# Tensor work of GpSimd before the first feed-forward moved to VectorE, in a two-block transformer kernel

## The chip, the cores and the metric

The kernel runs on one core of a Trainium2 chip. The metric is the device time of one execution in microseconds (us). Engines are named as in the profile: PE (matrix engine), PEld (its weight loads), DVE (VectorE), ACT (ScalarE), POOL (GpSimd), SP (issues most of the DMAs).

## The reference, cut

Two blocks work on 256 tokens of width 2048 in float32. What follows is the part around the change: the state-space mixer and the gated sum of the first block.

```python
def _s5_mixer(u, a_re, a_im, log_dt, b_re, b_im, c_re, c_im, d, w_glu):
    dt = jnp.exp(log_dt.astype(f32))[:, None]
    mag = jnp.exp(a_re * dt)
    abar_re = mag * jnp.cos(a_im * dt)
    abar_im = mag * jnp.sin(a_im * dt)
...
    bbar_re = z_re[..., None] * b_re - z_im[..., None] * b_im
    bbar_im = z_re[..., None] * b_im + z_im[..., None] * b_re
...
    y = (jnp.einsum('sbgn,gcn->bsgc', h_re, c_re.astype(f32))
         - jnp.einsum('sbgn,gcn->bsgc', h_im, c_im.astype(f32))
         + d.astype(f32) * uf)
    y = jax.nn.gelu(y.reshape(B, S, SSM_WIDTH))
    return y * jax.nn.sigmoid(y @ w_glu.astype(f32))

def first_block(...):
    cond = jax.nn.silu(c)
    mod = cond @ w_ada[i] + b_ada[i]
    shift1, scale1, gate1, shift2, scale2, gate2 = jnp.split(mod, N_MOD, axis=-1)
    h = _modulate(_rms(x, norm1_w[i]), shift1, scale1).astype(x.dtype)
    u, q, k, v = jnp.split(h @ w_in[i], splits, axis=-1)
    y_ssm = _s5_mixer(u, ...)
    y_att = _dilated_attention(q, k, v, q_norm_w[i], k_norm_w[i])
    mixed = jnp.concatenate([y_ssm, y_att], axis=-1).astype(x.dtype) @ w_out[i]
    x = x + gate1[:, None, :] * mixed
    h2 = _modulate(_rms(x, norm2_w[i]), shift2, scale2).astype(x.dtype)
    ffn = (jax.nn.silu(h2 @ w_ffn_gate[i]) * (h2 @ w_ffn_up[i])) @ w_ffn_down[i]
    return x + gate2[:, None, :] * ffn
```

The second block (neighbourhood attention, latent attention, attention to a memory of 256 tokens, a second feed-forward) follows; the keys and values of the memory are computed at the very start.

## The kernel before

All weights are streamed once, as tiles of 1 MB in one fixed order (`fl.order`), by SP into six buffers `r`. There are two kinds. A tile of kind "w" holds four chunks of 128 rows by 512 columns; it is split into a high and a low float32r part, in two halves: ACT writes `h` (L207), then `l = r - h` is made (L208). Four buffers each of `h` and `l`, of half a tile, stand between the splitters and PE. Each tile then costs PE 24 matmuls of 512 columns (`mm3`: L221, L222 with `h`, L226 with `l`). A tile of kind "a" is one of 96 tiles of `w_ada`; DVE alone takes it, with two multiply-adds into `acc` (L950), and PE needs it only when a half vector is done.

`Flow.run` sets the program order. For each "w" tile it emits the split of both halves, then the matmuls of an earlier tile, then one step of every open task (`fl.step`): the state-space tables (`s_prep`, at a rate of 1, later 2, then 3 steps per tile), the runs of the state-space sections (`s_run`), attention heads, norms and the ends of column groups. The schedule is manual, so every engine works through its own list in the order in which this code emits it, and waits at the head of its list.

Before the first feed-forward (some 84 "w" tiles and 84 "a" tiles) `Flow.share` says how many halves of a "w" tile get their low part on POOL: none for the memory's keys and values, then `(1,0)`, one half of every second tile, then `(1,)`, one half of every tile, up to the feed-forward, which has `(0,)`.

In the same stretch POOL makes the state-space tables in `Ssm.prep`, for each of eight sections: products of B and C with powers (L627, which read tables that ACT fetches), their sums into `X` and `C` (L635), three doublings of the rotation table `E` (`double`, L609 to L612; its first eight columns, `E8`, are made the same way once for all sections), the diagonal `dI` (L682), a zeroed `T` (L685). PE transposes `X` (L672), ACT copies the result (L673) and the first eight columns of `E` (L676), which the doublings then read. In `out1`, POOL multiplies the attention half of the output projection by the gate (L1194) and adds it to x (L1197). Further POOL work: zeroing `acc` (L945), ahead of a small DMA that ACT issues (L946), and the powers that make each reciprocal root (L299).

Of the kernel before, what the change touches and what calls it, by code (L numbers as in the profile page):

```python
# [13 lines left out]
OP = mybir.AluOpType  # L14
AX = mybir.AxisListType
PSUM = bass.MemoryType.PSUM
# [7 lines left out]
SP = 4  # L24
# [4 lines left out]
# ---------------------------------------------------------------- layout on the host  # L29
# [119 lines left out]
# ---------------------------------------------------------------- the program  # L149

class Core:
# [26 lines left out]
    # -- tiles  # L178
# [23 lines left out]
    def split_half(self, r, i, shared):  # L202
        """two float32r parts of two chunks of 128 rows of a weight tile of four"""
        nc = self.nc
        h, l = [self.wp.tile([128, 2, r.shape[-1]], F32R, name=self.nm(n), tag=n, bufs=self.NW) for n in "hl"]
        r = r[:, 2 * i:2 * i + 2]
        nc.scalar.activation(h, r, AF.Copy)  # L207
        (nc.gpsimd if shared else nc.vector).tensor_tensor(l, r, h.bitcast(F32), op=OP.subtract)  # L208
        return h, l

    def mm3(self, ps, acts, parts, first, last, ts=(0, 1)):
        """ps[t] += acts.T @ weights over two chunks; acts: [(h, l)], parts: (h, l) of the weights"""
        nc = self.nc
        if not isinstance(ps, list):
            ps = [ps[:, t] for t in range(2)]
        h, l = parts
        n = h.shape[-1]
        for k, (ah, al) in enumerate(acts):
            for t in ts:
                s = slice(t * 128, (t + 1) * 128)  # L220
                nc.tensor.matmul(ps[t][:, :n], al[:, s], h[:, k], start=first and k == 0, stop=False)  # L221
                nc.tensor.matmul(ps[t][:, :n], ah[:, s], h[:, k], start=False, stop=False)  # L222
        for k, (ah, al) in enumerate(acts):
            for t in ts:
                s = slice(t * 128, (t + 1) * 128)
                nc.tensor.matmul(ps[t][:, :n], ah[:, s], l[:, k], start=False,  # L226
                                 stop=last and k == len(acts) - 1)

    # -- to channel-major
    def tr4(self, src, k, dg=None):  # L230
        """chunks k, k+1 of token-major src (two tiles of [128, 512]) -> PSUM [128, 2, 256];
        dg: a diagonal matrix of factors for each token half"""
        ps = self.pm((128, 2, 256))
        for j in range(2):
            for t in range(2):
                o, i = ps[:, j, t * 128:(t + 1) * 128], src[t][:, (k + j) * 128:(k + j + 1) * 128]
                if dg is None:
                    self.nc.tensor.transpose(o, i, self.ident)  # L238
                else:
                    self.nc.tensor.matmul(o, i, dg[t], start=True, stop=True)  # L240
        return ps
# [4 lines left out]
    def chunks(self, src, n=4, w=None, ab=None, dg=None):  # L246
        """token-major src -> n chunks (h, l) of [128 channels, 256 tokens]; w(k): a factor per
        channel, ab(k): a factor and an offset per channel"""
        nc = self.nc
        out = []  # L250
        for k in range(0, n, 2):
            ps = self.tr4(src, k, dg)
            h, l = self.acts2()
            if w is None and ab is None:
                self.split(ps, h, l)
            for j in range(2):
                if w is not None:
                    self.split(ps[:, j], h[:, j], l[:, j], w(k + j))
                elif ab is not None:
                    a, b = ab(k + j)  # L260
                    f = self.up.tile([128, 256], F32, name=self.nm("f"), tag="f", bufs=3)
                    nc.scalar.activation(h[:, j], ps[:, j], AF.Identity, scale=a, bias=b)
                    nc.scalar.activation(f, ps[:, j], AF.Identity, scale=a, bias=b)
                    nc.vector.tensor_tensor(l[:, j], f, h[:, j].bitcast(F32), op=OP.subtract)
                out.append((h[:, j], l[:, j]))
        return out
# [10 lines left out]
    def plain(self, src, w=1.0, new=None):  # L277
        """token-major src -> two float32 tiles [128, 2, 256] of two chunks each"""
        out = []
        for k in (0, 2):  # L280
            ps = self.tr4(src, k)
            o = (new or self.unit)((128, 2, 256))
            self.nc.scalar.activation(o, ps, AF.Copy, scale=w)
            out.append(o)
        return out

    # -- norms
# [5 lines left out]
    def rstd(self, ss, n, width, out=None):  # L293
        """(ss / width + eps) ** -0.5 of n columns"""
        nc = self.nc
        r = self.small(n) if out is None else out
        m = self.small(n)
        nc.vector.tensor_scalar(m, ss, 1.0 / width, EPS, op0=OP.mult, op1=OP.add)  # L298
        nc.gpsimd.tensor_tensor(r, m, self.mhalf[:, :n], op=OP.pow)  # L299
        return r  # L300
# [6 lines left out]
    # -- attention pieces  # L307
    def softmax(self, src, scale):
        """src [128 queries, 2, 256 keys] -> normalised probabilities of softmax(scale * src)"""
        nc = self.nc  # L310
# [12 lines left out]
    def flip(self, p, parts=False):  # L323
        """probabilities -> [128 keys, 2, 256 queries], or two float32r parts of that"""
        nc = self.nc
# [13 lines left out]
    def values(self, ps, v, c, pt):  # L339
        """ps [128 channels, 256 queries] = v[:, c-th 128 columns].T @ probabilities"""  # L340
        for s in range(2):
            self.nc.tensor.matmul(ps, v[s][:, c * 128:(c + 1) * 128], pt[:, s], start=s == 0, stop=s == 1)  # L342


class Flow:
    """Streams the weight tiles in a fixed order, loads ahead, and steps the other tasks in between."""
# [36 lines left out]
    def run(self, main, other):  # L383
        """main: a generator that takes a split weight tile at each step; other[kind]: one that takes a raw tile"""
# [36 lines left out]
def pipeline(gens):  # L421
    """starts a generator at each step, with the earlier ones a step further"""
# [14 lines left out]
# ---------------------------------------------------------------- state space mixer  # L437

class Ssm:
# [17 lines left out]
    def params(self):  # L457
        """[128, 32] tables of one value per state; on VectorE and GpSimd"""
# [143 lines left out]
    def double(self, E, pr, steps):  # L602
        """powers of the rotation, from n = 2 ** i of them to twice as many: E[n:2n] = E[0:n] * ph[i]"""
        G, m = self.k.nc.gpsimd, E.shape[2]
# [12 lines left out]
    def prep(self, s):  # L617
        """the section's matmul operands and rotation tables"""
        k, nc, pool = self.k, self.k.nc, self.pool
        G, A = nc.gpsimd, nc.scalar  # L620
# [4 lines left out]
        def products(o, a, b):  # L625
            """a * b for four values b per state, a [128, SP, 16] -> a compact [128, SP, 4, 16]"""
# [4 lines left out]
        def combine(o, u, v, op):  # L631
            """each group of a pair to its own channels"""
# [52 lines left out]
        G.memset(T, 0.0)  # L685
# [6 lines left out]
    def finish(self):  # L692
        """the matmuls of the section whose tables were made last"""
# [18 lines left out]
    def run(self, s, u4, ytok):  # L712
        """u4 [128 (q, channel), SP, 64]; ytok: two views [128, 32 * SP], gelu(y) token-major"""
# [40 lines left out]
# ---------------------------------------------------------------- the two blocks  # L754

def build(ctx, tc, A, out):
# [23 lines left out]
    # ---- the order of the weight tiles  # L780
# [8 lines left out]
    def mixed(ws, as_, lag=0, lead=0):  # L789
        """weight tiles with the others spread evenly among all but the first and last of them"""  # L790
# [52 lines left out]
    # ---- groups of 512 columns  # L843
    open_ps = {}

    def group(acts, done, kbs, key=None, first=True, last=True, half=None):
        """takes a weight tile for each of kbs; acts[kb]: its four chunks, once there; then done(ps) is a task,
        or half(ps, t) ends each token half"""
# [18 lines left out]
    def tok(ps, r=None, n=512, base=None, new=unit):  # L867
        """a group's PSUM to two token-major tiles, times r per token, or added to those of base"""
# [15 lines left out]
    # ---- start: the memory, the input's norm  # L884
# [19 lines left out]
    def s_mem():  # L904
        """steps with the first weight tiles"""
# [31 lines left out]
    # ---- modulation  # L937
# [3 lines left out]
    def s_ada():  # L941
        """takes the tiles of w_ada in the order of W: 8 of two chunks to a half of a vector"""
# [42 lines left out]
    def modulate(xs, g, i, dg=None):  # L985
        """chunks of (x * r) * md[i + 1] + md[i] of the column group"""
# [27 lines left out]
    # ---- block 1: projections  # L1014
# [114 lines left out]
    # ---- block 1: state space mixer  # L1129
# [45 lines left out]
    # ---- block 1: output and feed-forward  # L1175
# [6 lines left out]
    def out1(g, i):  # L1182
        def done(ps):
            if i == 0:
                part[g] = tok(ps)
            elif i == 1:
# [6 lines left out]
                for t in range(2):  # L1193
                    G.tensor_tensor(part[g][t], part[g][t], gate[2][g], op=OP.mult)  # L1194
                yield
                for t in range(2):
                    G.tensor_tensor(x[g][t], x[g][t], part[g][t], op=OP.add)  # L1197
# [69 lines left out]
    # ---- block 2: mixers  # L1267
# [14 lines left out]
    def apply_rope(src, dst, nh, t):  # L1282
        """src, dst [128, nh, 64]"""
# [165 lines left out]
    # ---- block 2: memory attention  # L1449
    def parts(src, shape=(128, 2, 256)):  # L1450
        """a tile in two float32r parts"""
# [67 lines left out]
    def half2(ps, t):  # L1519
        """the last sum of a token half, and its norm"""  # L1520
# [16 lines left out]
    # ---- the program  # L1537
    fn = []

    def main():  # L1540
# [10 lines left out]
        fl.share = (1,0)  # L1551
# [13 lines left out]
        fl.share = (1,)  # L1565
# [73 lines left out]
```

## Time and profile before

| | us |
|---|---|
| median of 3 runs | 2764.36 (2763.05 to 2769.06) |
| span of the profiled execution | 2763.5 |
| PE busy | 2641.9 (96%) |
| DVE busy | 1665.0 (60%) |
| ACT busy | 1259.9 (46%) |
| POOL busy | 452.3 (16%) |
| chain that ended last: PE, POOL, DVE | 80%, 7%, 5% |

Busy times are averages over stages that differ: POOL's work lies nearly all in the first 750 us. The mean of a group of instructions includes any time in which an instruction had begun and was held up. Rows of waits name who ended the wait, not who caused it to be late. The profiled execution's span and the median differ by 0.9 us.

### The profile page before, as it was taken

Reading aid. Unit: us, or ns where it says so; the run is one execution under the profiler, and the core shown is the slowest. Engines: PE = TensorE matmul, PEld = TensorE weight load, DVE = VectorE, ACT = ScalarE, POOL = GpSimd, SP = SyncE. Lnnn points to the kernel's source line nnn. Section 1 sums busy time; section 2 is a strip of 40 time slices with the busy share of each in tenths; the row PEclk is TensorE's granted clock in tenths of the full one; section 3 lists DMA queues with packets and bytes.
Section 4 is the critical chain, followed back from the end, with each engine's and each line's share of the span. In section 5 each row is a group of like instructions: output and inputs, shape, how many; then the busy total and the mean of one; then the engine's idle time right before and its main releaser. Section 6 shows DMA issues by size and latency. Waiting matters only on the chain.

```text
span 2763.5 us, 31609 instructions
## 1 busy us (share of the span) xinstructions
PE 2641.9 (96%) x12272; PEld 2195.8 (79%) x12272; DVE 1665.0 (60%) x1834; ACT 1259.9 (46%) x1786; POOL 452.3 (16%) x409
## 2 busy tenths in 40 slices
PE   7879888888899999999999999999999999999998
PEld 6768777776788888888888878888888888888887
DVE  7967878769767554455456454665554454454445
ACT  5354445553544443433445455454454344443434
POOL 2470198827400000000000011100000000000001
PEclk9989999989999999999999999999999999999999
DMA  8978666557577555555545543455455555555552
GB/s 333 358 260 327 230 234 218 198 211 275 207 312 277 211 184 197 195 186 197 184 178 181 192 141 134 171 188 193 182 199 183 196 196 185 198 184 198 183 187 103
DMA packets 90030, 577.97 MB, mean 209 GB/s; under 512 B 9996, under 2 KB 12428, under 8 KB 22680
## 3 DMA queue, kind: packets, MB, share of 16 engines
q1 hardware_dynamic: 80928, 561.61, 55.2%
q10 hardware_dynamic: 8952, 14.34, 1.6%
q8 instruction: 96, 1.57, 0.2%
q14 instruction: 54, 0.44, 0.1%
HBM read 569.63 MB, written 6.29 MB: 208 GB/s over the span
## 4 chain that ended last, share of the span: by engine, by line
PE 80%; POOL 7%; DVE 5%; issue 3%; ACT 3%; DMA 1%; SPq 0%; ACTq 0%; POOLq 0%; DVEq 0%
PE g L226 25%; PE g L221 24%; PE g L222 24%; PE m L238 2%; DVE l L208 1%; POOL v L627 1%; DVE acc L950 1%; POOL l L208 1%; ACT h L207 1%; POOL C L635 1%; POOL X L635 1%; POOL v L609 1%; POOL v L610 1%; POOL u L1197 0%; POOL u L611 0%
## 5 line engine op out<-in xcount | busy, mean ns | idle before, releaser
L208 DVE TENSOR_TENSOR l<-r,h 128x1024 fp32r<-128x1024 f32 (+1 forms) x832 | 1025.9, 1266 | 587.9 <-ACT h L207 581.9
L221 PE MATMUL g<-h,u 128*128 128x512 f32 x3424 | 1357.1, 396 | 10.3 <-ACT h L207 8.2
L222 PE MATMUL g<-h,u 128*128 128x512 f32 x3424 | 1340.8, 392 | 0.0
L207 ACT ACTIVATE h<-r 128x1024 fp32r<-128x1024 f32 x866 | 884.6, 1056 | 668.7 <-PE g L222 601.0
L226 PE MATMUL g<-l,u 128*128 128x512 f32 x3424 | 924.4, 392 | 58.5 <-DVE l L208 39.6
L226 PEld LDWEIGHTS g<-l,u 128*128 128x128 f32 x3424 | 643.3, 189 | 204.4 <-DVE l L208 49.9
L221 PEld LDWEIGHTS g<-h,u 128*128 128x128 f32 x3424 | 650.4, 190 | 146.3 <-ACT h L207 10.9
L222 PEld LDWEIGHTS g<-h,u 128*128 128x128 f32 x3424 | 650.0, 190 | 132.9 <-issue 1.0
L950 DVE SCALAR_TENSOR_TENSOR acc<-r,cond,acc 128x1024 f32<-128x1024 f32 x192 | 280.6, 1461 | 3.6
L299 POOL TENSOR_TENSOR r<-s,mhalf 128x2 f32<-128x2 f32 x5 | 3.5, 702 | 894.8 <-DVE s L298 894.8
L208 POOL TENSOR_TENSOR l<-r,h 128x1024 fp32r<-128x1024 f32 x34 | 95.3, 2805 | 169.1 <-ACT h L207 164.9
L1515 POOL TENSOR_TENSOR u<-u,w 128x512 f32<-128x512 f32 x6 | 7.7, 1297 | 698.7 <-ACT j L291 698.7
L271 ACT ACTIVATE u<-m 128x512 fp32r<-128x512 f32 (+1 forms) x80 | 42.7, 574 | 162.8 <-PE m L238 128.3
L291 ACT ACTIVATE j<-u 128x512 bf16<-128x512 f32 (+2 forms) x92 | 47.3, 514 | 123.8 <-DVE u L1208 36.7
L272 DVE TENSOR_TENSOR u<-m,u 128x512 fp32r<-128x512 f32 (+1 forms) x80 | 50.0, 658 | 86.2 <-ACT u L271 86.2
L238 PE MATMUL m<-ident,u 128*128 128x128 f32 x372 | 53.3, 287 | 25.3 <-ACT u L982 11.9
L274 ACT ACTIVATE u<-m,vec 128x256 fp32r<-128x256 f32 x86 | 38.9, 472 | 72.7 <-PE m L342 30.5
L238 PEld LDWEIGHTS m<-ident,u 128*128 128x128 f32 x372 | 45.7, 148 | 32.7 <-ACT u L982 13.6
L275 DVE SCALAR_TENSOR_TENSOR u<-m,vec,u 128x256 fp32r<-128x256 f32 x86 | 40.0, 481 | 44.4 <-ACT u L274 44.3
L320 POOL TENSOR_TENSOR u<-u,s 128x512 f32<-128x512 f32 x20 | 20.8, 1042 | 265.4 <-DVE s L319 265.4
L1255 DVE TENSOR_TENSOR w<-g,w 128x512 f32<-128x512 f32 x24 | 16.5, 687 | 43.4 <-PE g L226 43.4
L1239 DVE SCALAR_TENSOR_TENSOR w<-g,r,w 128x512 f32<-128x512 f32 x22 | 15.5, 747 | 44.4 <-PE g L226 44.4
(238 smaller groups left out, 1438.5 us busy)
## 6 DMA issues: line engine op xcount, KB each, us to landing
r<-in_w_ada_dram SPq DMA_DIRECT2D x96, 1024.0 KB, 5.3
r<-in_wg_dram SPq DMA_DIRECT2D x88, 1024.0 KB, 4.8
r<-in_wu_dram SPq DMA_DIRECT2D x88, 1024.0 KB, 4.8
r<-in_wd_dram SPq DMA_DIRECT2D x88, 1024.0 KB, 4.8
r<-in_w_in_dram SPq DMA_DIRECT2D x32, 1024.0 KB, 4.9
r<-in_w_out_dram SPq DMA_DIRECT2D x32, 1024.0 KB, 6.1
r<-in_w_qkv_dram SPq DMA_DIRECT2D x24, 1024.0 KB, 4.8
r<-in_w_xk_dram SPq DMA_DIRECT2D x16, 1024.0 KB, 9.4
```

The costliest lines, as they stand in the source:

```text
L207: nc.scalar.activation(h, r, AF.Copy)
L208: (nc.gpsimd if shared else nc.vector).tensor_tensor(l, r, h.bitcast(F32), op=OP.subtract)
L221: nc.tensor.matmul(ps[t][:, :n], al[:, s], h[:, k], start=first and k == 0, stop=False)
L222: nc.tensor.matmul(ps[t][:, :n], ah[:, s], h[:, k], start=False, stop=False)
L226: nc.tensor.matmul(ps[t][:, :n], ah[:, s], l[:, k], start=False, stop=last and k == len(acts) - 1)
L238: self.nc.tensor.transpose(o, i, self.ident)
L271: nc.scalar.activation(h, ps, AF.Copy)
L272: nc.vector.tensor_tensor(l, ps, h.bitcast(F32), op=OP.subtract)
L275: nc.vector.scalar_tensor_tensor(l, ps, w, h.bitcast(F32), op0=OP.mult, op1=OP.subtract)
L291: self.nc.scalar.activation(j[:, :n], src, AF.Square, accum_out=acc)
L635: G.tensor_tensor(o[r, :, :, 16 * q:16 * q + 16], u[r], v[r], op=op)
L950: V.scalar_tensor_tensor(acc, r[:, j], cond[:, 2 * kb + j:2 * kb + j + 1], acc, op0=OP.mult, op1=OP.add)
```

## The change

Four edits. `split_half` keeps its branch, but `fl.share` is now `(0,)` in both places, so that DVE makes every low part. `double` and `prep` bind `G` to VectorE in place of GpSimd; zeroing `T` stays on GpSimd. In `out1` the gate's product and the sum go from `G` to `V`. Comments and docstrings are dropped as well.

```diff
     def double(self, E, pr, steps):
-        G, m = self.k.nc.gpsimd, E.shape[2]
+        G, m = self.k.nc.vector, E.shape[2]
...
     def prep(self, s):
         k, nc, pool = self.k, self.k.nc, self.pool
-        G, A = nc.gpsimd, nc.scalar
+        G, A = nc.vector, nc.scalar
...
         T = k.unit((128, SP, 128))
-        G.memset(T, 0.0)
+        nc.gpsimd.memset(T, 0.0)
...
                 for t in range(2):
-                    G.tensor_tensor(part[g][t], part[g][t], gate[2][g], op=OP.mult)
+                    V.tensor_tensor(part[g][t], part[g][t], gate[2][g], op=OP.mult)
                 yield
                 for t in range(2):
-                    G.tensor_tensor(x[g][t], x[g][t], part[g][t], op=OP.add)
+                    V.tensor_tensor(x[g][t], x[g][t], part[g][t], op=OP.add)
...
         m_acts.clear()
-        fl.share = (1,0)
+        fl.share = (0,)
         prep[1] = 3
...
             yield from group(mixed_acts, out1(g, 0), (2,))
-        fl.share = (1,)
+        fl.share = (0,)
         for g in range(2):
```

PE's and ACT's lists stay the same, word for word. On DVE, in the middle of the projections, this is where one section's rotation table is doubled (`u_4568` is that section's `E`, `csl` and `snl` are cosines and sines, `l` a low part):

```order
 L950 SCALAR_TENSOR_TENSOR acc_4052<-r_4355,cond,acc_4052 128x1024 x2
 L208 TENSOR_TENSOR l_4536<-r_4359,h_4535 128x1024
+L208 TENSOR_TENSOR l_4540<-r_4359,h_4539 128x1024
+L609 TENSOR_TENSOR v_4570<-u_4568,csl 128x64
+L610 TENSOR_TENSOR v_4571<-u_4568,snl 128x64
+L611 TENSOR_TENSOR u_4568<-v_4570,v_4571 128x4x8
+L612 TENSOR_TENSOR u_4568<-v_4570,v_4571 128x4x8
+L609 TENSOR_TENSOR v_4576<-u_4568,csl 128x128
+L610 TENSOR_TENSOR v_4577<-u_4568,snl 128x128
```

The second half's low part and the doublings now stand in DVE's list, between one tile's low parts and the next; L609 there waits for ACT's copy L676, as it did on POOL.

On POOL, this is the place of the first norm's reciprocal root (`r_107`, L299), between two sections' tables:

```order
-L612 TENSOR_TENSOR u_1615<-v_1671,v_1672 128x4x32
-L682 TENSOR_TENSOR v_1677<-i_119,ssm_p 128x128
 L685 MEMSET u_1679 128x512
 L299 TENSOR_TENSOR r_107<-s_1687,mhalf 128x2
-L627 TENSOR_TENSOR v_1731<-u_1729,wr 128x256
-L627 TENSOR_TENSOR v_1732<-u_1729,wi 128x256
-L635 TENSOR_TENSOR X<-v_1731,v_1732 64x16x16 x2
-L627 TENSOR_TENSOR v_1813<-u_1729,wi 128x256
-L627 TENSOR_TENSOR v_1814<-u_1729,wr 128x256
-L635 TENSOR_TENSOR X<-v_1813,v_1814 64x16x16 x2
 L945 MEMSET acc_1876 128x1024
```

Only the zeroing of `T` and `acc` and the root remain there.

On DVE, at the end of the output projection (`u_5325`, `u_5327` are x, the other `u` parts and gates, `g_5369` a group's PSUM):

```order
 L208 TENSOR_TENSOR l_5393<-r_5265,h_5392 128x1024
+L208 TENSOR_TENSOR l_5397<-r_5265,h_5396 128x1024
+L1197 TENSOR_TENSOR u_5325<-u_5325,u_4680 128x512
+L1197 TENSOR_TENSOR u_5327<-u_5327,u_4681 128x512
+L1194 TENSOR_TENSOR u_4788<-u_4788,u_4849 128x512
+L1194 TENSOR_TENSOR u_4789<-u_4789,u_4849 128x512
 L1189 TENSOR_TENSOR u_4851<-g_5369,u_4851 128x512
 L1189 TENSOR_TENSOR u_4852<-g_5369,u_4852 128x512
```

The gated sums stand between a tile's low parts and the next group's sum.

## Rows read from the trace of the kernel before

**Rows 1.** Stages: us; busy us (count) of PE, PEld, DVE, ACT, POOL; PEclk, DMA
```profile
0.00:110.00 110.00, 90.34 (x402) 72.14 (x403) 92.23 (x181) 51.12 (x77) 29.34 (x36) 0.98 0.91 341
110.00:750.00 640.00, 552.14 (x2695) 459.73 (x2694) 501.77 (x547) 307.19 (x564) 366.26 (x306) 0.93 0.66 246
...
750.00:2760.00 2010.00, 1999.41 (x9179) 1663.96 (x9178) 1070.97 (x1108) 901.56 (x1145) 56.72 (x67) 1.00 0.52 190
```

**Rows 2.** Waits in 0 to 750 us: who for whom, us in total, times, longest
```profile
PE g L226 <- DVE l L208: 39.1, 19, 5.1
...
ACT h L207 <- POOL acc L945: 33.7, 3, 20.1
...
DVE u L724 <- PE m L721: 30.9, 5, 12.1
...
PE g L226 <- POOL l L208: 18.9, 5, 8.5
...
PE m L238 <- ACT u L982: 11.9, 5, 8.3
ACT u L982 <- POOL r L299: 11.1, 1, 11.1
...
PE g L221 <- ACT h L207: 8.2, 4, 4.0
...
PE m L672 <- POOL X L635: 5.2, 2, 3.5
```

**Rows 3.** PE's waits in 0 to 110 us
```profile
PE g L226 <- DVE l L208: 11.0, 7, 3.4
```

**Rows 4.** DVE by form in 0 to 750 us: count | busy us, mean ns | idle before
```profile
L950 DVE SCALAR_TENSOR_TENSOR acc<-r,cond,acc 128x1024 f32<-128x1024 f32 x162 | 242.1, 1495 | 3.0
L208 DVE TENSOR_TENSOR l<-r,h 128x1024 fp32r<-128x1024 f32 x140 | 202.4, 1477 | 36.8 <-ACT h L207 36.6
L732 DVE TENSOR_TENSOR_SCAN u<-m,u 128x64 f32<-128x64 f32 x64 | 21.2, 399 | 0.0
L264 DVE TENSOR_TENSOR u<-f,u 128x256 fp32r<-128x256 f32 x28 | 11.7, 425 | 33.5 <-ACT f L263 33.5
L1208 DVE TENSOR_TENSOR u<-u,u 128x512 f32<-128x512 f32 x8 | 8.8, 1102 | 0.8
...
L726 DVE TENSOR_TENSOR u<-u,u 128x256 f32<-128x256 f32 x8 | 5.5, 688 | 0.3
L724 DVE TENSOR_TENSOR u<-m,u 128x512 f32<-128x512 f32 x8 | 5.5, 686 | 30.9 <-PE m L721 30.9
L725 DVE TENSOR_TENSOR u<-m,u 128x512 f32<-128x512 f32 x8 | 5.4, 679 | 0.0
```

**Rows 5.** The same two forms on DVE in 760 to 1000 us, with POOL idle
```profile
L208 DVE TENSOR_TENSOR l<-r,h 128x1024 fp32r<-128x1024 f32 x88 | 104.8, 1221 | 48.7 <-ACT h L207 48.0
L950 DVE SCALAR_TENSOR_TENSOR acc<-r,cond,acc 128x1024 f32<-128x1024 f32 x28 | 35.9, 1281 | 0.5
```

**Rows 6.** POOL's timeline, 319 to 330 us: start, us, instruction [idle before]
```profile
321.34 2.98 POOL L208 TENSOR_TENSOR l<-r,h 128x1024 fp32r<-128x1024 f32 x1 [10.11 <-ACT h L207]
```

**Rows 7.** DVE's timeline in the same stretch
```profile
319.49 2.58 DVE L950 SCALAR_TENSOR_TENSOR acc<-r,cond,acc 128x1024 f32<-128x1024 f32 x2
321.99 4.55 DVE L208 TENSOR_TENSOR l<-r,h 128x1024 fp32r<-128x1024 f32 x2
326.46 1.55 DVE L732 TENSOR_TENSOR_SCAN u<-m,u 128x64 f32<-128x64 f32 x8
```

**Rows 8.** POOL by form in 0 to 750 us, columns as in Rows 4
```profile
L208 POOL TENSOR_TENSOR l<-r,h 128x1024 fp32r<-128x1024 f32 x34 | 95.3, 2805 | 169.1 <-ACT h L207 164.9 <-issue 3.9
L635 POOL TENSOR_TENSOR C<-v,v 64x256 f32<-64x256 f32 x32 | 36.4, 1137 | 2.2
...
L1194 POOL TENSOR_TENSOR u<-u,u 128x512 f32<-128x512 f32 x8 | 16.4, 2075 | 3.0 <-DVE u L1189 3.0
...
L609 POOL TENSOR_TENSOR v<-u,csl 128x64 f32<-128x64 f32 x8 | 8.0, 1003 | 7.5 <-ACT u L676 7.3
```

## The prediction

> **What bounds the kernel now.** I read the stages first. From 750 us on PE is busy for 1999 of 2010 us and POOL for 57 [rows 1]; the change touches nothing there, so those 2010 us stay. Before that PE is not the bound: from 110 to 750 us it is busy for 552 of 640 us, which leaves 88 us idle, and its granted clock is 0.93. Of its two levels, 2.4 and 1.2 GHz, it has thus the lower one for about 14% of that stretch, while after 750 us it is 1.00. POOL works for 366 us there, DVE for 502 [rows 1]. In 0 to 110 us POOL has 29 us, and DMA engines are at 0.91: little can change there.
>
> Next, who ends PE's waits [rows 2]. Low parts from DVE lead with 39.1 us, of which 11.0 lie ahead of 110 us [rows 3]. Low parts from POOL have 18.9, with one wait of 8.5. POOL also stands behind three names that don't show it at once. X (L635) for the transposes ends 5.2 us. The 11.9 us for ACT's L982 come from a root that lies in POOL's list behind a section of tables: ACT itself waited 11.1 us for POOL's r (L299). And the 8.2 us for the high part L207 go with ACT's 33.7 us of waits for POOL's zeroed acc (L945), which blocks ACT's list at the small DMA behind it. All in [rows 2].
>
> Third, DVE itself. Its two great forms take 1495 ns (L950) and 1477 ns (L208) in 0 to 750 us [rows 4], and 1281 and 1221 ns in 760 to 1000 us, when POOL does nothing [rows 5]. One place shows why. A low part on POOL runs from 321.34 us for 2.98 us [rows 6], and DVE's two low parts that begin at 321.99 take 4.55 us together [rows 7], where two clean ones take 2.4 by [rows 5]. Nor is it all of DVE: the products that read PSUM (L724, L725) stay at 686 and 679 ns, while L1208 of the same size, with both inputs in SBUF, has 1102 [rows 4]. So a DVE instruction with two SBUF inputs stands still while POOL reads.
>
> The Trainium skill states this rule: by "SBUF — State Buffer", section Who interferes with whom, a VectorE instruction with two SBUF inputs and a GpSimd instruction that reads SBUF exclude each other for the whole instruction. The trace agrees, with the 1102 against 679 ns just named.
>
> **The change part by part.** Time that DVE gets back, from the difference of means: L950 162 x (1495 - 1281) ns = 34.7 us; L208 140 x (1477 - 1221) = 35.8 us [rows 4, 5]. The scans L732 take 21.2 us for 64, or 331 ns each; a clean run of eight takes 1.55 us, 194 each [rows 4, 7], so 64 x 137 = 8.8 us. Seven more lines have two SBUF inputs; priced like L1208 against L725 (8 x 423 ns = 3.4 us, three lines of 512) and L726 against L264 (8 x 263 ns = 2.1 us, four of 256) they give at most 18.6, of which I take 15. Sum 94 us.
>
> Work that DVE takes on. 34 low parts [rows 8] at 104.8/88 = 1.19 us [rows 5] make 40.5 us. The 16 gated products and sums (L1194 has 8 [rows 8]; L1197 as many) at L725's 5.4/8 = 0.675 us make 10.8. Of the tables, eight sections and E8 (the same doublings, once for all states) have 146 instructions of 256 columns (64 products, 64 sums over 64 partitions, 18 in doublings) and 98 of 128 columns or fewer. At L264's 11.7/28 = 0.418 us [rows 4] the wide ones make 61.0. The narrow ones cost between nothing and 0.418 us, 0 to 41 us; I take half, 20.5, since they have a fourth to a half of L264's columns or fewer. Sum 133 us, between 112 and 153. POOL's own time for such work is no measure of it: its low part takes 2805 ns and its L635 1137 ns, waits for DVE included [rows 8].
>
> So DVE's busy time in 0 to 750 us goes from 92 + 502 = 594 us to about 594 - 94 + 133 = 633 us, **39 us more** (18 to 59). It still has 750 - 633 = 117 us free.
>
> What PE gets back, in 110 to 750 us: the waits for POOL's low parts, 18.9; for X, 5.2; for L982, 11.9, since the root finds POOL's list empty and memsets alone are ahead of it; for the high parts 8.2 [rows 2], since acc is zeroed early. Of DVE's 39.1 - 11.0 = 28.1 us half, 14, as its low parts are no longer stretched (from none to all: 0 to 28). Sum 58 us of the 88 us idle. The clock follows: 0.07 of 640 us, 45 us, are lost to the lower level, which goes with PE's idle times, since it is 1.00 where PE is busy throughout [rows 1]; a share of 58/88 gives 30 us. Together 88 us.
>
> Against this stands DVE's longer list. I charge the whole net 39 us to the end, since DVE is the one that PE then waits for and its list is taken in order; were it all hidden in DVE's free time, it would cost nothing. The ends of the added work move this to 18 or 59.
>
> A rule that speaks against the change is in "Perfetto Trace Analysis", section Optimizing Scalar/DVE Operations, of the Trainium skill: with a saturated VectorE, handing work to another engine, GpSimd even, may pay; the page adds that between these two it might not, as they share a read port. By the rule alone DVE would be charged with 133 us, without the 94; by the rows it is charged with 39.
>
> Edits with one answer: the zeroing of T stays on POOL; the small DMA of biases and the weight tiles keep their queues; SP waits for buffers freed by the low parts, and these come no later than now if DVE keeps up.
>
> **The sum.** 2763.5 - 58 - 30 + 39 = 2714.5 us of span, and with the 0.9 us between span and median **2715 us**. With the charge at 18 or 59 and the half of DVE's waits at all or none (14 either way), it lies between 2680 and 2749.
>
> **The rivals.**
> First, DVE's added work is hidden. DVE had 750 - 594 = 156 us free [rows 1] against 39 more. Then the gain is the 88 us and up to 14 more: 2662 to 2676 us. For it speaks that most of that free time is spent behind ACT or PE, which speed up; against it that tables come in bursts of several us between two tiles, and PE has but two tiles of split weights ahead of it.
>
> Second, and this ends on the other side, the tables stall DVE. POOL could wait for ACT's copy of E without harm, and did for 7.5 us [rows 8]; now L609 waits at the head of DVE's list, with the low parts of the next tile and L950, which frees SP's buffers, queued behind. ACT's copy lies behind its copy of the transposes (L673), these behind PE's matmuls of a tile. DVE has such a wait already: L724 waits for PE, 30.9 us in 5 waits, 6.2 on average and 12.1 at the longest [rows 2]. The gain of 49 us is gone at 49/8 = 6.1 us for each of eight sections; with 6.2 the result is no change, about 2765 us, and with 12.1 for each, 97 us, it is 2812. Against it: PE is no later than now, and when DVE is the late one, ACT and PE are through before it comes to L609.
>
> Third, the blocked time isn't POOL's doing, and doesn't come back: then the charge is 133 instead of 39, and 2715 + 94 = 2809 us. L724 and L725 speak against it [rows 4].
>
> That the change doesn't do what it says is no rival: POOL's list keeps memsets and roots alone in this stretch.
>
> **How the numbers follow.** Forecast 0.60, spread over 2680 to 2749; the hidden work 0.17; the stall of sections 0.20, half of it near no change and half beyond it; blocked time that stays 0.03. A difference under 0.2%, 5.5 us, is about what a measurement of this kernel can't tell from none. Faster by more: 0.60 + 0.17 + 0.01 of the stall's lower end = 0.78; within: 0.09; slower: 0.10 + 0.03 = 0.13. The range goes from 2668, which leaves out part of the first rival, to 2775, which leaves out most of the slower cases: together 0.18.
>
> **What would show it.** In 0 to 750 us POOL's tensor work is gone; the means of L950 and L208 on DVE are those of [rows 5]; DVE's busy sum up to the same point of the program is near 633 us; the waits of PE for POOL and of ACT for acc are gone, and PEclk is nearer to 1. The first feed-forward begins some 50 us earlier. If L609 or L627 on DVE show long waits for ACT, or PE's waits for DVE's low parts rise beyond 39 us, the second rival has come; if the means of L950 and L208 stay, the third.

## The result and the profile after

The changed kernel takes 2724.94 us (median of 4 runs, 2723.84 to 2726.3), the kernel before beside it 2765.78 us. The ratio is 0.9848, with a 95% interval of 0.9837 to 0.9859: 42 us, or 1.5%, faster. The forecast was 2715 us, 49 us faster. The spans of the two profiled executions are 2721.8 and 2763.5 us.

Stages of the changed kernel, columns as in [rows 1]:

```profile
0.00:110.00 110.00, 94.90 (x418) 75.68 (x419) 92.92 (x183) 52.15 (x78) 21.99 (x26) 0.98 0.92 346
110.00:710.00 600.00, 536.65 (x2701) 447.08 (x2701) 528.86 (x842) 309.05 (x572) 24.57 (x22) 0.96 0.70 264
...
750.00:2715.00 1965.00, 1957.16 (x8976) 1629.14 (x8975) 1037.06 (x1073) 876.43 (x1114) 56.19 (x67) 1.00 0.51 188
```

The gain lies all ahead of the first feed-forward, which PE reaches about 40 us earlier. Against [rows 1], where that stretch ends at 750 us: PE was busy for 90.3 + 552.1 = 642.5 us and idle for 107.5; now, up to 710 us, it is busy for 631.6 and idle for 78.4. So of 40 us some 29 are PE's idle time and 11 are the same matmuls in less busy time, with a granted clock of 0.96 in place of 0.93. DVE is busy for 92.9 + 528.9 = 621.8 us, 28 more than the 594 before, in 40 us less.

DVE by form in the changed kernel, 0 to 710 us, columns as in [rows 4]:

```profile
L950 DVE SCALAR_TENSOR_TENSOR acc<-r,cond,acc 128x1024 f32<-128x1024 f32 x162 | 207.4, 1280 | 3.3
L208 DVE TENSOR_TENSOR l<-r,h 128x1024 fp32r<-128x1024 f32 x174 | 204.7, 1218 | 12.4 <-ACT h L207 12.2
L635 DVE TENSOR_TENSOR C<-v,v 64x256 f32<-64x256 f32 x32 | 13.4, 420 | 0.8
...
L732 DVE TENSOR_TENSOR_SCAN u<-m,u 128x64 f32<-128x64 f32 x64 | 12.4, 264 | 0.0
...
L1208 DVE TENSOR_TENSOR u<-u,u 128x512 f32<-128x512 f32 x8 | 5.5, 692 | 0.3
...
L1194 DVE TENSOR_TENSOR u<-u,u 128x512 f32<-128x512 f32 x8 | 5.1, 683 | 0.0
...
L609 DVE TENSOR_TENSOR v<-u,csl 128x64 f32<-128x64 f32 x8 | 1.7, 218 | 0.0
```

Each of the long forms is back at its clean time: L950 went from 1495 to 1280 ns and L208 from 1477 to 1218, against 1281 and 1221 in [rows 5], L1208 from 1102 to 692 [rows 4]. 174 low parts now take 204.7 us, where 140 took 202.4. The last row is the first step of each section's doublings, behind ACT's copy of `E`: DVE had no idle time ahead of its eight instances.

PE's waits in the changed kernel, 0 to 710 us, columns as in [rows 2], and two of ACT's behind them:

```profile
PE g L226 <- DVE l L208: 39.3, 24, 4.5
PE m L238 <- DMA u<-in_mem_dram: 7.8, 4, 4.5
PE g L221 <- ACT h L207: 6.2, 4, 2.8
PE m L238 <- ACT u L982: 5.3, 6, 2.6
PE m L1105 <- ACT u L1101: 5.1, 2, 3.8
```
```profile
ACT u L982 <- POOL r L299: 4.7, 1, 4.7
...
ACT u L875 <- POOL acc L945: 3.1, 1, 3.1
```

Against [rows 2]: POOL's low parts (18.9 us) and X (5.2) no longer stop PE, L982 went from 11.9 to 5.3, the high parts from 8.2 to 6.2. DVE's low parts are where they were, 39.1 then and 39.3 now, in 24 shorter waits instead of 19.

### The profile page after: what moved, and what is told of

It reads as the page before. It is cut to its first block, busy times and chain, and to the rows that moved or that the text cites. A ratio compares the mean times of both kernels' runs of the same rounds, so it can differ in the third digit from the quotient of the medians.

```text
span 2721.8 us, 31521 instructions
## 1 busy us (share of the span) xinstructions
PE 2628.7 (97%) x12272; PEld 2184.9 (80%) x12272; DVE 1691.5 (62%) x2128; ACT 1258.8 (46%) x1786; POOL 103.2 (4%) x115
## 4 chain that ended last, share of the span: by engine, by line
PE 79%; DVE 11%; issue 7%; ACT 2%; DMA 1%; POOL 0%; SPq 0%; ACTq 0%; DVEq 0%; POOLq 0%
PE g L226 25%; PE g L221 24%; PE g L222 24%; DVE l L208 3%; DVE acc L950 2%; PE m L238 2%; DVE v L627 1%; ACT h L207 0%; PE m L342 0%; DVE u L732 0%; PE m L1488 0%; PE m L1475 0%; DVE C L635 0%; PE m L240 0%; PE m L329 0%
## 5 line engine op out<-in xcount | busy, mean ns | idle before, releaser
L208 DVE TENSOR_TENSOR l<-r,h 128x1024 fp32r<-128x1024 f32 x866 | 1028.2, 1222 | 562.5 <-ACT h L207 554.9
L226 PE MATMUL g<-l,u 128*128 128x512 f32 x3424 | 922.1, 391 | 39.9 <-DVE l L208 39.7
L226 PEld LDWEIGHTS g<-l,u 128*128 128x128 f32 x3424 | 642.5, 189 | 185.2 <-DVE l L208 52.4
L221 PEld LDWEIGHTS g<-h,u 128*128 128x128 f32 x3424 | 648.0, 189 | 144.8 <-ACT h L207 10.3
L950 DVE SCALAR_TENSOR_TENSOR acc<-r,cond,acc 128x1024 f32<-128x1024 f32 x192 | 245.8, 1280 | 3.8
L272 DVE TENSOR_TENSOR u<-m,u 128x512 fp32r<-128x512 f32 (+1 forms) x80 | 50.0, 658 | 85.5 <-ACT u L271 85.4
L238 PEld LDWEIGHTS m<-ident,u 128*128 128x128 f32 x372 | 45.6, 147 | 24.2 <-ACT u L982 6.8
L1255 DVE TENSOR_TENSOR w<-g,w 128x512 f32<-128x512 f32 x24 | 16.5, 687 | 43.4 <-PE g L226 43.4
L299 POOL TENSOR_TENSOR r<-s,mhalf 128x2 f32<-128x2 f32 x5 | 4.4, 889 | 1010.1 <-DVE s L298 1010.1
L1237 DVE TENSOR_TENSOR w<-g,w 128x512 f32<-128x512 f32 x22 | 14.2, 685 | 44.3 <-PE g L226 44.3
L1511 DVE TENSOR_TENSOR u<-g,u 128x512 f32<-128x512 f32 x22 | 14.2, 685 | 44.3 <-PE g L226 44.3
L1231 ACT ACTIVATE w<-g,r 128x512 f32<-128x512 f32 x22 | 13.9, 686 | 52.9 <-PE g L226 52.9
```

The lines of the kernel that those rows point to most:

```text
L272: nc.vector.tensor_tensor(l, ps, h.bitcast(F32), op=OP.subtract)
L950: V.scalar_tensor_tensor(acc, r[:, j], cond[:, 2 * kb + j:2 * kb + j + 1], acc, op0=OP.mult, op1=OP.add)
```

## The experiments

A ratio is to the kernel before on the same chip; differences in us are differences of ratios times 2767 us.

**One part at a time.** Three kernels, each with one part of the change and the other two undone.

```diff
 # only_low, against the changed kernel
-        G, m = self.k.nc.vector, E.shape[2]
+        G, m = self.k.nc.gpsimd, E.shape[2]
...
-        G, A = nc.vector, nc.scalar
+        G, A = nc.gpsimd, nc.scalar
...
-                    V.tensor_tensor(part[g][t], part[g][t], gate[2][g], op=OP.mult)
+                    G.tensor_tensor(part[g][t], part[g][t], gate[2][g], op=OP.mult)
```

> One part alone: the 34 low parts go to VectorE, tables and gated sums stay on GpSimd. Theory A (GpSimd's reads hold up VectorE, and GpSimd's late results hold up PE): VectorE takes on 40.5 us and gets back the low parts' share of the 94 us, 95 of 395 us of GpSimd's time, so 23; PE loses its 18.9 us of waits for GpSimd's low parts. 10 to 25 us faster than before, about 2745. Theory B (only how VectorE is loaded counts, GpSimd's slowness is beside the point): VectorE has 40 us more to do, 0 to 15 us slower.

Measured 2743.54 us, ratio 0.9912 (0.9899 to 0.9926): 24 us faster. Theory B falls. DVE takes on 34 low parts and is not busier for it (589.7 us up to the first feed-forward, at 730 us here, against 594 before), since its instructions shrink, as three forms show (0 to 750 us):

```profile
L208 DVE TENSOR_TENSOR l<-r,h 128x1024 fp32r<-128x1024 f32 x183 | 239.4, 1349 | 36.2 <-ACT h L207 36.0
L950 DVE SCALAR_TENSOR_TENSOR acc<-r,cond,acc 128x1024 f32<-128x1024 f32 x168 | 230.9, 1375 | 3.2
L732 DVE TENSOR_TENSOR_SCAN u<-m,u 128x64 f32<-128x64 f32 x64 | 15.4, 310 | 0.0
```

By [rows 4], 162 x (1495 - 1375) + 140 x (1477 - 1349) ns + (21.2 - 15.4) us of scans give 43 us, as much as the 34 low parts cost. Their share of what DVE gets back had been put at 23 us, about half of that.

```diff
 # only_tables, against the changed kernel
-        fl.share = (0,)
+        fl.share = (1,0)
         prep[1] = 3
...
-        fl.share = (0,)
+        fl.share = (1,)
         for g in range(2):
...
-                    V.tensor_tensor(part[g][t], part[g][t], gate[2][g], op=OP.mult)
+                    G.tensor_tensor(part[g][t], part[g][t], gate[2][g], op=OP.mult)
```

> One part alone: the state-space tables go to VectorE; every low part that was on GpSimd stays there, gated sums too. Theory A: VectorE takes on 81 us and gets back some 55 of the 94 us; the waits for X, for the root and for the zeroed acc go. 5 to 25 us faster than before. Theory B: VectorE has 80 us more to do, slower by 10 us or more.

Measured 2751.61 us, ratio 0.9942 (0.9929 to 0.9954): 16 us faster. Here DVE does pay: L950 still takes 1462 ns and L208 1401, the low parts on POOL 2883. By the same sum DVE gets back 162 x 33 + 140 x 76 ns + 8.8 us of scans = 25 us, where 55 had been put, and it is busy for 641.8 us up to the first feed-forward (736 us here), 48 more than before. PE's waits say how it came out ahead all the same (0 to 735 us):

```profile
PE g L226 <- DVE l L208: 54.7, 30, 5.1
PE m L238 <- DMA u<-in_mem_dram: 8.6, 4, 4.0
PE g L226 <- POOL l L208: 7.0, 3, 3.6
PE m L238 <- ACT u L982: 4.8, 6, 2.6
```

PE waits 16 us longer for DVE's low parts than in [rows 2], but 12 less for POOL's, which are no longer behind tables in POOL's list, 7 less for L982, and not at all for X (5 us). That is 8 us less in sum, of 11 by which PE's idle time falls (736 - 639.5 = 96.5 us, 107.5 before).

```diff
 # only_gate: the changed kernel with both fl.share as before, and
-        G, m = self.k.nc.vector, E.shape[2]
+        G, m = self.k.nc.gpsimd, E.shape[2]
...
-        G, A = nc.vector, nc.scalar
+        G, A = nc.gpsimd, nc.scalar
```

> One part alone: the 16 gated products and sums go to VectorE. Theory A: they cost GpSimd 2.1 us each with VectorE standing still, and VectorE 0.68; 3 to 10 us faster than before, all of it at the end of the output projection. Theory B: 0 to 5 us slower.

Measured 2764.2 us, ratio 0.9985 (0.9976 to 0.9994): 4 us faster, the sign and the size that theory A gave, though small. The three parts give 24 + 16 + 4 = 44 us, the whole change 42: within their intervals they add.

**Reads on POOL that nobody waits for.** The cause by itself, without any late result. `ident` is the 128 x 128 identity; the scratch of the tables has three buffers in place of four, which makes room for `eb`.

```diff
+    def extra(self):
+        a = self.ident.unsqueeze(1).to_broadcast([128, 2, 128])
+        for _ in range(4):
+            self.nc.gpsimd.tensor_tensor(self.eb, a, a, op=OP.add)
...
                     main.send(split.pop(0))
+                    if self.nth < 84:
+                        k.extra()
                     self.step()
```

> The changed kernel with work on GpSimd that nobody waits for: at each of 84 weight tiles four sums of a 256-column view of the identity, written to a tile of its own (one buffer fewer in the tables' scratch pays for it). Theory A: GpSimd's reads hold up VectorE. It has at least 210 us of them; before, 366 us came with 94 us of stretched VectorE time, so 50 us or more, charged to the end: 25 to 60 us slower than the changed kernel, with the means of L950 and L208 (here shifted by a few lines) well above 1280 and 1220 ns. Theory C (before was slow because PE and ACT waited for GpSimd's results, and VectorE's stretch was harmless): within 5 us of the changed kernel.

Measured 2797.68 us, ratio 1.0108 (1.0092 to 1.0123): 72 us slower than the changed kernel, beyond what theory A gave, and slower than the kernel before. DVE's list is the changed kernel's, its instructions are longer. DVE (0 to 750 us), then POOL (0 to 800 us), then PE's longest row of waits (0 to 760 us); L213, L958 and L231 are L208, L950 and L226 here:

```profile
L213 DVE TENSOR_TENSOR l<-r,h 128x1024 fp32r<-128x1024 f32 x168 | 226.1, 1387 | 5.7 <-ACT h L212 5.7
L958 DVE SCALAR_TENSOR_TENSOR acc<-r,cond,acc 128x1024 f32<-128x1024 f32 x160 | 220.9, 1381 | 3.2
```
```profile
L177 POOL TENSOR_TENSOR eb<-ident 128x256 f32<-128x256 f32 x332 | 327.6, 987 | 24.1
```
```profile
PE g L231 <- DVE l L213: 78.1, 34, 7.4
```

PE's wait for low parts is 78.1 us, against 39.3: 39 of the 45 us by which PE's idle time grows (782 - 658.3 = 123.7 us, 709 - 630.5 = 78.5 in the changed kernel). The rest of the 72 us is PE's busy time, 28 us more for the same matmuls. Theory C falls: stretched DVE time alone is costly. Up to the first feed-forward (782 us here by the difference of spans, 709 in the changed kernel) DVE is busy for 94.0 + 617.5 = 711.4 us instead of 621.4:

```profile
0.00:110.00 110.00, 81.26 (x311) 63.11 (x312) 93.96 (x132) 43.58 (x68) 84.65 (x92) 0.89 0.75 278
110.00:782.00 672.00, 577.03 (x2801) 475.09 (x2800) 617.45 (x891) 316.46 (x579) 288.52 (x288) 0.93 0.66 245
sum 782.00, PE 658.29 PEld 538.20 DVE 711.41 ACT 360.04 POOL 373.18; mean PE 329.15 PEld 269.10 DVE 355.70 ACT 180.02 POOL 186.59
```

**The control: POOL writes and does not read.** The fills stand where the sums stood; the rest of the edit is that of pool_reads.

```diff
+    def extra(self):
+        for _ in range(9):
+            self.nc.gpsimd.memset(self.eb, 0.0)
```

> The control to pool_reads: the changed kernel with nine fills of the same tile on GpSimd in the place of the four sums, about 2.4 us per weight tile, at the same places of the program and with one buffer fewer in the tables' scratch. It writes and reads nothing. Theory A (GpSimd's reads hold up VectorE): within 5 us of the changed kernel, 2720 to 2730, and the means of L950 and L208 stay near 1280 and 1220 ns. Rival D (any work on GpSimd delays its roots and fills, or the smaller scratch costs something): 20 us slower or more, as with the sums, which took 73.

Measured 2726.37 us, ratio 0.9855 (0.9841 to 0.9868), the changed kernel's time. Its forms on DVE (L957 and L212 are L950 and L208), then its fills on POOL, 0 to 710 us:

```profile
L957 DVE SCALAR_TENSOR_TENSOR acc<-r,cond,acc 128x1024 f32<-128x1024 f32 x162 | 207.3, 1280 | 3.2
L212 DVE TENSOR_TENSOR l<-r,h 128x1024 fp32r<-128x1024 f32 x174 | 204.7, 1218 | 13.0 <-ACT h L211 12.8
```
```profile
L176 POOL MEMSET eb<- 128x256 f32 x747 | 233.3, 312 | 41.4
```

233 us of fills stretch neither of these forms. Rival D falls: neither a busy POOL nor the smaller scratch costs anything that the time shows. What the sums do and the fills don't is to read SBUF; that it is the reading, and nothing else in a sum, rests on this pair of runs.

**What DVE's list costs, downwards.** The tables' arithmetic is left out; their tiles hold zeros.

```diff
-            G.tensor_tensor(o, a.unsqueeze(2).to_broadcast([128, SP, 4, 16]), ...)
+            pass
...
-                G.tensor_tensor(o[r, :, :, 16 * q:16 * q + 16], u[r], v[r], op=op)
+            pass
...
+        nc.gpsimd.memset(E[:, :, :, 8:64], 0.0)
         A.activation(E[:, :, :, 0:8], self.E8[:, :, pr], AF.Copy)
-        self.double(E, pr, (3, 4))
-        self.double(E, pr, (5,))
...
+        nc.gpsimd.memset(dI, 0.0)
```

> The changed kernel without the arithmetic of the state-space tables (products, sums, doublings, diagonal left out; the tiles are zeros, filled by GpSimd), so that the scan works on zeros. VectorE loses some 70 us of the 622 that it is busy before the first feed-forward. Theory A, with every us that VectorE takes on charged to the end: 45 to 75 us faster than the changed kernel, 2650 to 2680. Rival (the added work lies in VectorE's free time): within 15 us of the changed kernel.

Measured 2684.8 us, ratio 0.9704 (0.9689 to 0.9719): 40 us faster than the changed kernel, between the two. Up to the first feed-forward DVE is busy for 548.6 us, 73 less than the changed kernel's 621.4, whose sum stands second:

```profile
sum 670.00, PE 613.03 PEld 513.15 DVE 548.56 ACT 360.99 POOL 51.29; mean PE 306.51 PEld 256.57 DVE 274.28 ACT 180.49 POOL 25.64
```
```profile
sum 709.00, PE 630.54 PEld 521.95 DVE 621.36 ACT 360.19 POOL 46.56; mean PE 315.27 PEld 260.98 DVE 310.68 ACT 180.10 POOL 23.28
```

40 of 73 us, a bit more than half of what the tables cost DVE, reach the end. By the two rows, 21 us of them are PE's idle time (670 - 613.0 = 57.0 us, against 78.5) and 18 its busy time.

**And upwards.**

```diff
-            G.tensor_tensor(o, a.unsqueeze(2).to_broadcast([128, SP, 4, 16]), ...)
+            for _ in range(3):
+                G.tensor_tensor(o, a.unsqueeze(2).to_broadcast([128, SP, 4, 16]), ...)
```

> The changed kernel with each of the 64 products of the tables (L627, 0.42 us) made three times over on VectorE, the same result written again: 128 instructions of 256 columns more, some 45 to 53 us of VectorE's list. It measures the charge from the other side of no_tables, where 70 us less gave 40. If VectorE's list is the bound wherever tables stand in it: 35 to 55 us slower than the changed kernel, about 2770. If as much of it hides as there (a half or more): 20 to 30 us slower, about 2750.

Measured 2782.15 us, ratio 1.0053 (1.0036 to 1.007): 57 us slower than the changed kernel. DVE's busy time up to the first feed-forward rises by 676.0 - 621.4 = 55 us, and as much reaches the end:

```profile
sum 768.00, PE 655.17 PEld 540.57 DVE 675.98 ACT 361.74 POOL 46.61; mean PE 327.58 PEld 270.28 DVE 337.99 ACT 180.87 POOL 23.31
```

It isn't one for one, though: PE's idle time grows by 34 us (768 - 655.2 = 112.8), its busy time by 25, with the granted clock at 0.92 from 110 us on in place of 0.96. By these two runs the changed kernel stands at a bend: further table work on DVE costs about its whole time, a good part of it through the clock, and table work taken away gives about half.

**The place of the zeroed acc.** Here the kernel before has one edit:

```diff
-            G.memset(acc, 0.0)
+            V.memset(acc, 0.0)
```

> The kernel before, with the 12 fills of acc on VectorE in place of GpSimd, nothing else. It takes ACT's 33.7 us of waits for the zeroed acc away and leaves GpSimd's tensor work and VectorE's stretch. If the place of the fills in GpSimd's list counted as forecast (8.2 us of PE's waits for high parts, and clock with it): 5 to 12 us faster than before. If ACT's waits were idle time that nobody needed: within 4 us.

Measured 2777.16 us, ratio 1.0038 (1.0025 to 1.005): 10 us slower, which neither side gave. ACT's waits for acc did not go, they grew from 33.7 to 56.5 us:

```profile
ACT h L207 <- DVE acc L945: 56.5, 9, 15.0
PE g L226 <- DVE l L208: 42.4, 27, 4.9
```

On DVE the fill stands behind low parts and multiply-adds, and ACT's small DMA waits behind it as before. So this kernel doesn't show what ACT's wait was worth; it only shows that such a wait, made longer, costs PE time (its waits for high parts are 21.6 us here, 8.2 in [rows 2]). Nor are the 10 us that wait's alone: DVE's list has the fills on top, and DVE is busy for 605.5 us up to the first feed-forward (761 us here), 11.5 more than before.

**Three tries at a better kernel.** First, the gated sum in one product.

```diff
-                    V.tensor_tensor(part[g][t], part[g][t], gate[2][g], op=OP.mult)
-                yield
-                for t in range(2):
-                    V.tensor_tensor(x[g][t], x[g][t], part[g][t], op=OP.add)
...
-        m = unit()
-        V.tensor_tensor(m, ps, gate[2][g], op=OP.mult)
+        m = part[g][t]
+        V.tensor_tensor(m, ps, m, op=OP.add)
+        V.tensor_tensor(m, m, gate[2][g], op=OP.mult)
```

> The changed kernel with the gated sum written in one piece: the attention half is added to the last PSUM and the sum multiplied by the gate once, so that L1194 and L1197 (16 instructions, 10 us) go and 8 sums come at the end. VectorE loses net 5 us. If VectorE is the bound up to the end of the output projection: 3 to 8 us faster than the changed kernel; if the last token half's one more sum counts instead, 0 to 2 us slower.

Measured 2720.25 us, ratio 0.9831 (0.9818 to 0.9844): 5 us faster than the changed kernel by the ratios, as expected of work taken from DVE. The intervals overlap, so it is the fastest kernel here, but not by a clear margin.

Second, one_product with smaller bursts of table work.

```diff
-        prep[1] = 3
+        prep[1] = 2
```

> one_product with two steps of the tables per weight tile in the place of three, so that VectorE has smaller bursts of table work between two tiles. If bursts cause the waits of PE for low parts that came with the change: 3 to 10 us faster than one_product (2720). If VectorE's total counts: within 3 us; if sections come late for their runs: slower.

Measured 2721.59 us, ratio 0.9834 (0.982 to 0.9849): no change in sum. PE's waits for DVE's low parts did fall, from 35.1 to 30.2 us, but those for two other names grew by 11 (L1101 from 5.1 to 10.0, L736 from 3.4 to 9.8), so this run doesn't show that bursts cost nothing.

Third, one_product with the multiply-adds of w_ada between the two low parts. In the changed kernel four of them in a row hold up a low part; DVE's timeline shows it, and PE's L226 begins at 515.18 us after 4.51 us of waiting:

```profile
508.75 5.24 DVE L950 SCALAR_TENSOR_TENSOR acc<-r,cond,acc 128x1024 f32<-128x1024 f32 x4
513.91 2.35 DVE L208 TENSOR_TENSOR l<-r,h 128x1024 fp32r<-128x1024 f32 x2
```

```diff
             if kind != "w":
-                other[kind].send(r)
+                held.append((kind, r))
                 continue
...
                 n += 1
+                if held:
+                    kind, r2 = held.pop(0)
+                    other[kind].send(r2)
```

> one_product with the two multiply-adds of a w_ada tile (2.6 us) put between the two halves of the next weight tile's low parts, so that never four of them stand in a row ahead of a low part, as at 508.75 us of the changed kernel, where PE waits 4.5 us. VectorE's total is the same. If where the long instructions stand counts: 3 to 12 us faster than one_product. If only the total counts: within 3 us.

Measured 2739.34 us, ratio 0.9899 (0.9884 to 0.9914): 19 us slower than one_product. PE's waits for DVE's low parts did shrink, from 35.1 us to 23.4, but a tile that waits in its buffer keeps SP from the next load: SP's waits for L950 went from 442.4 to 535.6 us. ACT now waits for weights, 24.2 and 14.6 us in the first and third row, where one_product has 13.9 and 4.2:

```profile
ACT h L207 <- DMA r<-in_w_in_dram: 24.2, 6, 5.9
PE g L226 <- DVE l L208: 23.4, 27, 2.7
...
ACT h L207 <- DMA r<-in_w_xk_dram: 14.6, 6, 4.5
```

## Why the prediction was right, point by point

**Time that DVE gets back, 94 us: right.** By the rows of after, L950 gives 162 x 215 ns = 35 us, L208 140 x 259 = 36, the scans 21.2 - 12.4 = 9, and the seven further lines, put at 15, give 14.9 (L1208 8.8 - 5.5 = 3.3, and so on). That POOL's work of this kind is the cause is shown by pool_reads and pool_writes; the third rival falls.

**Work that DVE takes on, 133 us: right, but DVE's net 39 us came as 28.** By the rows of after the 34 low parts take 40.0 us, the gated products and sums 10.3, the tables 85.4: 136. Summed over all rows of DVE by form up to the first feed-forward, its busy time goes from 618.4 to 656.7 us, 38 more, as forecast. DVE as a whole goes from 594 to 621.4, 27 more: instructions of different rows overlap, by 24 us before and by 35 after. That overlap stood in no term of the forecast. DVE's timeline of the changed kernel, columns as in [rows 6], shows two products of the tables one behind the other:

```profile
504.70 0.43 DVE L627 TENSOR_TENSOR v<-u,npr 128x256 f32<-128x256 f32 x1
505.05 0.42 DVE L627 TENSOR_TENSOR v<-u,pi 128x256 f32<-128x256 f32 x1
```

They begin 0.35 us apart and were charged 0.42 each.

**PE's waits, 58 us less 39 of charge, so 19 net: 29 came.** Of the names that should go, POOL's low parts and X went whole (24 us), L982 for 6.6 of 11.9, and the high parts for 2.0 of 8.2: ACT's waits for acc fell from 33.7 to 3.1 us, so that link from acc to PE was too strong, and acc_vector couldn't test it. DVE's low parts gave nothing in sum, 39.1 and 39.3 us, where 14 us of gain and 39 of charge, 25 more, had been forecast. That some waits went with the stretch and others came with the longer list is likely (no_tables, with neither, has 28.3 us) but isn't shown one by one; the two terms should have stood together.

**The clock, 30 us: mis-sized.** PE's busy time for the same matmuls fell by 11 us. That the clock goes with PE's idle time about held: of the 88 us idle from 110 us on, 25 came back (640 - 552.1 = 87.9, now 600 - 536.7 = 63.3), and that share of 45 us is 13. But the forecast took the share from the 58 us of waits that should go, and not from the 19 us left after the charge, though the charge is idle time of PE too. With 19/88 the term would have been 10 us.

So the total is partly luck. The clock came 19 us short, and PE's idle time fell by 10 more than forecast; together that is about what the change fell short by. With the clock taken from the net, the same working would have given about 2735 us.

**The charge at full price: too high, and not shown by the row it was argued from.** The whole net 39 us were charged as waits of PE. thrice_products shows 34 us of idle time for 55 us of DVE's, no_tables 21 for 73; only with the clock do they become about 59 and 39. For the net 28 us of DVE that is some 8 to 17 us of waits, by these two rates, in place of 39. The first rival, that the added work is hidden, falls: part of it was not.

**The stall of sections by ACT's copy of E: did not come.** L609 had no idle time ahead of it. ACT's copy was there each time DVE came to it, which was the argument against that rival.

## What to carry to other kernels

A busy share of 16% on GpSimd (here 395.6 of the first 750 us, 53%) can be dear when VectorE's instructions have two SBUF inputs: compare the mean of one VectorE form in stretches with and without GpSimd's work before work is shared out between them. Sums on GpSimd that read SBUF were not free though nobody waited for their results (72 us); fills were, within the noise. PE's idle time costs a second time through the clock, so take that term from the net. Before a list is reordered for an engine, look at the buffers that its instructions free.

## What had not been expected of the hardware

Per us of GpSimd's time, the low parts were dearer for VectorE than short instructions. L208, L950 and the scans together show it: only_low takes 34 low parts of 1024 columns, 95 us, from GpSimd and gives these three forms 43 us back, 0.45 us per us. only_tables takes 220 us of instructions with 256 columns or fewer (POOL is busy for 175.7 us in place of 395.6) and gives them 25 back, 0.11. The 332 sums of pool_reads, 328 us, cost them 174 x (1387 - 1218) + 162 x (1381 - 1280) ns + 1.5 us of scans = 47 us, 0.14; the rest of the 90 us by which VectorE is busier there (711.4 against 621.4) lies in its other instructions, the tables among them. Whether it is their length or their place isn't separated: low parts on GpSimd begin beside those on VectorE, at 321.34 and 321.99 us in [rows 6] and [rows 7].

Nor is it two SBUF inputs alone. A form with one SBUF input and a constant, in 0 to 110 us of the changed kernel, of pool_reads and of pool_writes:

```profile
L474 DVE TENSOR_SCALAR q<-q 128x224 f32<-128x224 f32 x12 | 3.3, 276 | 0.3
```
```profile
L482 DVE TENSOR_SCALAR q<-q 128x224 f32<-128x224 f32 x12 | 7.4, 618 | 0.3
```
```profile
L481 DVE TENSOR_SCALAR q<-q 128x224 f32<-128x224 f32 x12 | 4.1, 338 | 0.3
```

GpSimd's sums more than double it, and the fills stretch it too, by 62 ns. There are few such instructions in this kernel, so it hardly shows in the time.
